# Mixing layer in seven block products per pair of output chunks, with weight sums from DRAM and a fixed queue order into the up-projection

## The chip, the cores and the metric

The kernel runs on one core of a Trainium2 chip. The metric is the device time in microseconds (us) of one execution; lower is better. TensorE (PE) multiplies, VectorE (DVE), ScalarE (ACT) and GpSimd (POOL) do the elementwise work, and the SyncE queue (SP) issues most transfers. Each engine works through its own queue in the order in which the kernel's instructions stand there.

## The reference, cut to what matters

One layer of a hybrid decoder, all in float32, with 1024 tokens, a width of 1024 and a feed-forward width of 2816:

```python
xn = rmsnorm(x, norm_mix_w[l])
proj = xn @ w_in[l]
...
y_da = diff_attention(da_q, da_k, da_v, lam, lam_init, subln_w[l])
y_sw = sliding_window_attention(sw_q, sw_k, sw_v, sinks[l])
merged = jax.nn.sigmoid(g_da) * (y_da @ w_br_da[l]) + jax.nn.sigmoid(g_sw) * (y_sw @ w_br_sw[l])
x = x + merged @ w_mix_out[l]
xn = rmsnorm(x, norm_ffn_w[l])
x = x + conv_ffn(xn, w_up[l], conv_w[l], conv_b[l], w_down[l])
```

The change is about the line `x = x + merged @ w_mix_out[l]`, called mixing here, and about what stands on both sides of it: the merge of the two branches before, the first product of the up-projection (`up`) behind.

## The kernel before

Activations lie transposed: a matrix of 1024 x 1024 is eight chunks of 128 channels x 1024 tokens, and a half is 512 tokens of a chunk. Every float32 operand is split into a high part (a cast by ACT) and a low part (a subtraction by DVE: source less high part); a product of two blocks then takes three matmuls (high x high, high x low, low x high) of 128 x 128 against 128 x 512. In `mm3` these are L215, L216 and L217.

The stages are `project` (L315), `attention` (L544), and in `rest` (L819) the merge, then `mix` (L880), `hidden` with up (L960) and `down` (L1263). A pair of output chunks in project, up and down is already computed by seven block products instead of eight (a Strassen scheme): with the weights' blocks A11, A12, A21, A22 and the activations' blocks B11, B12, B21, B22, the products take sums of weight blocks (S1 to S4) and sums of activation blocks (T1 to T4). In project and up POOL makes the weight sums in SBUF; for down they are made in DRAM by `sums_of` (L82), with copies on SP's queue and accumulating transfers on POOL's.

*Merge.* For each of eight output chunks m, two gates are loaded (gr), multiplied by rstd on POOL (L846) and put through a sigmoid on ACT; PE multiplies the branch weights, DVE multiplies gate and product (L857 and L862), POOL adds the branches (L863, DVE for the last chunk), and the chunk is split (L866, L867) into the operands mh and ml.

*Mixing.* For each output chunk, in the order 0, 4, 1, 5, 2, 6, 3, 7, eight input chunks x two halves x three matmuls = 48 matmuls accumulate in PSUM (sc), DVE adds the result to the residual (L905), ACT stores it (x2d, a transfer issued from ACT's queue, L610), multiplies by the norm's weight (L908) and squares (L917), and POOL adds the squares up (L918, in the tile rstd). After every second chunk `operands` (L924) builds up's operands B11, B21, B22 and T13 from the pair (L943 to L947); T4 and T2 are left as sums in t42 tiles and are split at the start of up. The weights of a chunk are split by ACT (L194) and DVE (L196) ahead of the chunk. A scheduler places most of the instructions; `in_order` makes the instructions of its block keep the written order on the engines that it is given, and is used before from within up's first pair on.

*Start of up.* The column sums of the squares are matmuls against ones (L223); DVE makes the mean (ms, L230), POOL takes the power -0.5 (rs, L232), and PE spreads it over the partitions (L238). The products of up are `product` (L957). The weights of up's first pair are split in `split_pair` (L175).

## Time and profile before

| what | value |
|---|---|
| median of 3 runs (lowest to highest) | 1323.16 us (1323.06 to 1323.33) |
| profiled execution: its time, its span | 1323.83 us, 1322.0 us |
| granted TensorE clock over the span | 0.998 |
| busy PE, DVE, ACT, POOL | 1307.9, 1019.0, 658.0, 476.4 us |
| evictions of mixing (L905), first and last start | 599.5 and 675.7 us |

The page's engine row gives busy time, share of the span and instructions. PEld is the loading of weights, which overlaps the matmuls. In the view of waits a row names an engine and line, what it waited for, and then the total, the count and the longest one in us. In a windows table the engines stand as PE, PEld, DVE, ACT, POOL with their instructions in brackets, then the granted clock, the DMA share and GB/s. In a group of instructions the busy time and the mean in ns follow the bar; in the view of a line or tile it is the least, median and greatest duration in ns.

### The profile page before, as it was taken

The numbers are of one execution on the slowest core, as the hardware profiler recorded it, in microseconds if no ns is written. First come the engines' busy times: TensorE is split into PE (matmuls) and PEld (weight loads), VectorE is DVE, ScalarE is ACT, GpSimd is POOL, SyncE is SP. The second block draws the span as 40 slices with busy tenths as digits, with TensorE's granted clock in tenths as the row PEclk, the third lists the DMA queues.
The fourth block names the chain that finished last, engine by engine and source line by source line (L and its number), as shares of the span: only waits on it lengthen the run. The fifth ranks groups of instructions, "written<-read, shape, count | busy, mean of one in ns | idle before, by whom it ended". The sixth has DMA issues, their size and how long they took to land. (4 is left out here: it accounts for less than half of the span.)

```text
span 1322.0 us, 16947 instructions
## 1 busy us (share of the span) xinstructions
PE 1307.9 (99%) x6210; PEld 1089.6 (82%) x6210; DVE 1019.0 (77%) x1380; ACT 658.0 (50%) x1043; POOL 476.4 (36%) x364
## 2 busy tenths in 40 slices
PE   9999999999999999999999999999999999999997
PEld 7888888888888878888887888888888888888886
DVE  8847775289888976446678988888988898896855
ACT  8532232276667765334445545445454544554543
POOL 0446652000111015661427667656766632000002
PEclk9999999999999999999999999999999999999999
DMA  7344343976544236334433546745554127953534
GB/s 262 116 142 158 148 154 127 259 188 178 153 124 143 85 120 223 144 112 149 137 112 123 184 143 153 201 146 137 197 139 124 62 86 259 330 191 118 160 98 147
DMA packets 71586, 205.95 MB, mean 156 GB/s; under 512 B 8016, under 2 KB 15824, under 8 KB 71376
## 3 DMA queue, kind: packets, MB, share of 16 engines
q1 hardware_dynamic: 57472, 176.03, 40.7%
q0 software_dynamic: 2304, 11.54, 4.9%
q10 hardware_dynamic: 11728, 17.31, 3.6%
q8 instruction: 49, 0.80, 0.2%
q14 instruction: 33, 0.27, 0.1%
HBM read 156.08 MB, written 71.83 MB: 172 GB/s over the span
## 5 line engine op out<-in xcount | busy, mean ns | idle before, releaser
L1243 POOL TENSOR_TENSOR us<-us,rstd 128x1024 f32<-128x1024 f32 x42 | 105.3, 2507 | 145.6 <-DVE us L1168 109.8
L196 DVE TENSOR_TENSOR wl<-raw,wh 128x1024 fp32r<-128x1024 f32 (+2 forms) x85 | 97.5, 1148 | 58.8 <-ACT wh L194 49.2
L194 ACT CAST wh<-raw 128x1024 fp32r<-128x1024 f32 (+2 forms) x85 | 74.2, 874 | 120.2 <-PE y L1313 50.7
L145 DVE TENSOR_TENSOR sl<-sf,sh 128x1024 fp32r<-128x1024 f32 x42 | 105.2, 2506 | 3.4 <-ACT sh L138 3.4
L232 POOL TENSOR_TENSOR rs<-ms,mhalf 128x8 f32<-128x8 f32 (+2 forms) x9 | 14.2, 1576 | 240.3 <-DVE ms L230 234.1
L1180 DVE SCALAR_TENSOR_TENSOR c<-us,vecs,c 128x1024 f32<-128x1024 f32 x76 | 95.6, 1279 | 0.7
L1313 PE MATMUL y<-h,wh 128*128 128x512 f32 (+1 forms) x324 | 95.2, 377 | 0.0
L1313 PE MATMUL d<-h,wh 128*128 128x512 f32 x264 | 81.3, 389 | 0.0
L215 PE MATMUL g<-xh,wh 128*128 128x512 f32 x176 | 71.0, 404 | 1.5 <-ACT g L618 1.5
L217 PE MATMUL g<-xh,wl 128*128 128x512 f32 x176 | 70.3, 399 | 0.0
L216 PE MATMUL g<-xl,wh 128*128 128x512 f32 x176 | 70.3, 399 | 0.0
L1313 PEld LDWEIGHTS y<-h,wh 128*128 128x128 f32 x324 | 59.4, 188 | 11.1
L1313 PE MATMUL y<-h,wl 128*128 128x512 f32 (+1 forms) x162 | 60.9, 376 | 0.0
L693 DVE CUSTOM_DVE_ANT_0 L<-sc,bias 128x128 f32<-128x128 f32 (+7 forms) x64 | 47.7, 751 | 17.1 <-PE sc L689 14.0
L672 POOL MEMSET aT<- 128x128 f32 x32 | 6.2, 206 | 151.9 <-PE t L718 98.1
L694 ACT ACTIVATE L<-L,sm 128x128 f32<-128x128 f32 (+7 forms) x64 | 49.6, 778 | 19.9 <-DVE sm L693 17.3
L1313 PEld LDWEIGHTS d<-h,wh 128*128 128x128 f32 x264 | 49.6, 188 | 10.3
L846 POOL TENSOR_TENSOR gr<-gr,rstd 128x1024 f32<-128x1024 f32 x16 | 40.3, 2523 | 46.3 <-DMA gr<-gd 46.1
L1313 PE MATMUL d<-h,wl 128*128 128x512 f32 x132 | 51.5, 390 | 0.0
L138 ACT CAST sh<-sf 128x1024 fp32r<-128x1024 f32 x42 | 44.3, 1054 | 11.7 <-POOL sf L124 7.6
L216 PE MATMUL sc<-ml,wh 128*128 128x512 f32 x128 | 49.9, 390 | 0.0
L689 PE MATMUL sc<-u,u 128*128 128x512 f32 (+2 forms) x192 | 49.9, 359 | 0.0
(438 smaller groups left out, 4180.4 us busy)
## 6 DMA issues: line engine op xcount, KB each, us to landing
u<-qd SPq DMA_DIRECT2D x72, 256.0 KB, 6.5
raw<-in_w_up SPq DMA_DIRECT2D x23, 512.0 KB, 3.9
raw<-in_w_in SPq DMA_DIRECT2D x22, 512.0 KB, 3.7
hd<-c SPq DMA_DIRECT2D x22, 512.0 KB, 4.0
sdP<-in_w_down POOLq DMA_DIRECT2D x16, 704.0 KB, 8.6
rv<-in_w_up SPq DMA_DIRECT2D x21, 512.0 KB, 3.6
hc<-hd SPq DMA_DIRECT2D x33, 256.0 KB, 5.1
gr<-gd SPq DMA_DIRECT2D x16, 512.0 KB, 3.5
```

The lines of the kernel that those rows point to most:

```text
L145: self.nc.vector.tensor_tensor(lo, src, hi.bitcast(F32), ALU.subtract)
L194: self.hi = nc.scalar.copy(wh, raw)
L196: self.lo = (eng or nc.vector).tensor_tensor(wl, raw, wh.bitcast(F32), ALU.subtract)
L215: nc.tensor.matmul(ps, wh[:, kc + o, :], ah, start=first and n == 0, stop=False)
L216: nc.tensor.matmul(ps, wh[:, kc + o, :], al, start=False, stop=False)
L217: nc.tensor.matmul(ps, wl[:, kc + o, :], ah, start=False, stop=last and n == len(kcs) - 1)
L689: nc.tensor.matmul(sc[:, lo + n0:lo + n1], qs, k[c][part][:, n0:n1], start=part == 0, stop=part == 1)
L693: nc.vector.tensor_tensor_reduce(L[:, :w], sc[:, lo:lo + w], self.bias[:, o:o + w], slope, 3e38, ALU.add, ALU.min, s[:, 0:1])
L694: nc.scalar.activation(L[:, :w], L[:, :w], AF.Exp, bias=s[:, 0:1], scale=-1.0, accum_out=s[:, 1:2] if c else self.s0[:, i:i + 1])
L1180: nc.vector.scalar_tensor_tensor(c, us[:, 2 - n:T + 2 - n], cw[2 - n], c, ALU.mult, ALU.add)
L1243: i = (nc.vector if m % NF == 0 else nc.gpsimd).tensor_tensor(us[:, 2:], us[:, 2:], self.rstd, ALU.mult)
L1313: nc.tensor.matmul(ps, v[:, k - k0, :], x, start=start and k == i == 0, stop=k == HK - 1 and i == 2, skip_group_check=True)
```

## The change

Mixing goes over to seven products as well, for the pairs of output chunks (0, 4) and (1, 5), then (2, 6) and (3, 7). One product is 12 matmuls (four input chunks x three) into one half; there are 28 products, counted here 1 to 28 in the order in which PE takes them, 14 for each round. In a round with chunks a and b, two products share a weight unit: B11 and B21 of a (1, 2), of b (3, 4); T2 and T1 of a (5, 6), of b (7, 8); T3 and B22 of a (9, 10), of b (11, 12); T4 of a and b (13, 14). The second round has 15 to 28. Products of one chain accumulate in one bank of PSUM, and the bank's intermediate states are added to several output blocks.

- `mix_sums` makes the sums of w_mix in DRAM during project: 32 transfers of 256 KB, 16 copies on SP and 16 accumulating ones on POOL, four per pair.
- The merge runs over the chunks 0, 4, 1, 5, 2, 6, 3, 7, its gates lie in other buffers, and behind each second chunk `mix_operands` splits the six operands of the pair. In the last chunk DVE evicts and adds half by half.
- From the last merge chunk's second branch through mixing into up, `in_order` fixes DVE, ACT and POOL in the written order. Weights are prepared by `ahead(1)`, one unit ahead.
- In mixing, DVE adds one product in three to the residual tiles straight from PSUM; of the others ACT copies the bank and POOL adds (`copied`). Squares, stores (now by half chunks), norm weights, and up's operands (`put`, `t13`, `t4`) follow at once. The first pair of up is loaded, summed and split within the second round.
- up's first pair is computed in the fixed order, and `down` takes its buffers for loaded chunks from tiles that mixing left.

The core of the diff:

```diff
+    def mix_sums(self):
+        row = lambda m, r: self.w_mix[m].rearrange("p k c -> p (k c)")[:, r * H2:(r + 1) * H2]
+        copy = lambda n, src: lambda m: nc.sync.dma_start(self.sm[m][:, n], src(m))
+        add = lambda n, o, r: lambda m: nc.gpsimd.dma_start(self.sm[m][:, n], row(m + o, r), accum_op=ALU.add)
+        for step in (copy(1, lambda m: row(m + 4, 0)), copy(2, lambda m: row(m + 4, 0)), add(1, 4, 1), add(2, 0, 0),
+                     copy(0, lambda m: self.sm[m][:, 1]), add(0, 0, 0), copy(3, lambda m: self.sm[m][:, 0]), add(3, 0, 1)):
...
             for j, ms in enumerate(self.pairs):
                 w = self.next_w()
+                for _ in range(4):
+                    with tc.issue_after(self.sync), tc.issue_after(self.sum):
+                        next(sums, None)
...
-                for m in range(KC):
+                for m in self.mix_order:
...
-                    (nc.vector if m == KC - 1 else nc.gpsimd).tensor_tensor(gs[0], gs[0], gs[1], ALU.add)
-                    a = mp.tile([P, T], F32R, name=f"mh{m}")
-                    b = mp.tile([P, T], F32R, name=f"ml{m}")
-                    nc.scalar.copy(a, gs[0])
-                    nc.vector.tensor_tensor(b, gs[0], a.bitcast(F32), ALU.subtract)
+                    nc.gpsimd.tensor_tensor(gs[0], gs[0], gs[1], ALU.add)
+                    res[m] = gs[0]
+                    if m > 3:
+                        self.mix_operands(m - 4, "B11", "B21", "B22", "T13", "N2", "T4", ga=res[m - 4], gb=res[m])
+                self.last = {i.engine: None for i in (self.hi.ins, self.lo.ins, self.pow.ins)}
+                with self.in_order(self.last):
+                    ga, gb = res[3], gs[0]
+                    for hf in range(2):
...
+                        nc.vector.tensor_tensor(g, g, ps, ALU.mult)
+                        nc.vector.tensor_tensor(x, x, g, ALU.add)
...
+    def mix_operands(self, k, *names, ga, gb):
...
+        for name in names:
+            if name == "T13":
+                tt(b11, b11, b12, ALU.subtract)
+                tt(b12, b22, b12, ALU.subtract)
+            elif name == "N2":
+                stt(b22, b22, -1.0, b11, ALU.mult, ALU.subtract)
+            elif name == "T4":
+                stt(b21, b22, -1.0, b21, ALU.mult, ALU.subtract)
+            hi, lo = self.split(*self.M[name, k], {"B11": b11, "B21": b21, "B22": b22, "T13": ga, "N2": b22, "T4": b21}[name])
...
+        def post(m, hf):
+            x = h2(X[m], hf)
+            if hf in begun:
+                sq = self.tl(stp, [P, H2], "s")
+                nc.scalar.activation(sq, x, AF.Square)
+                gt(h2(acc, hf), h2(acc, hf), sq, ALU.add)
...
+            nc.scalar.dma_start(self.x2d[m, :, hf * H2:(hf + 1) * H2], x)
+            if m > 3:
+                norm_w(m, hf)
...
+        with self.in_order(self.last):
+            self.mix_operands(3, "B11", "B21", "B22", "T13", "N2", "T4", ga=ga, gb=gb)
...
+            for a in (0, 2):
...
+                wa = self.wq.pop(0)
+                c1[a] = bank(n1[0])
+                run(c1[a], wa, 0, "B11", True)
+                self.ahead(1)
...
+                run(c2[a], wa, 1, "B21", True)
+                copied(c1[a], a, 0)
+                wb = self.wq.pop(0)
...
+                tt(h2(X[b], 1), h2(X[b], 1), c3[b], ALU.add)
+                post(b, 1)
+                t13(a)
+                if a:
+                    put("B22", b, h2(t42[b], 1))
+                    self.low(pair, "g")
+                    self.sums(pair, "sb")
+                run(c1[b], v, 1, "T4", False)
...
-            with tc.high_priority(400):
-                w0 = self.split_pair(*pair)
+            with self.in_order(self.last):
+                self.whole(pair, "sa")
+                self.ends[0]()
+                self.whole(pair, "sb")
+                self.ends[1]()
+                self.whole(pair, "v")
+            w0 = pair["w"]
...
+                    order = self.in_order(self.last)
+                    order.__enter__()
                     for k in range(4):
                         hi, lo = self.split(*(xc2.tile([P, T], F32R, name=f"T42_{k}{p}") for p in "hl"), self.t42[k])
...
-                            with tc.high_priority(400):
-                                rs = self.rstd_cols(ssq, 8, D)
+                            rs = self.rstd_cols(ssq, 8, D)
+                    order.__exit__(None, None, None)
```

How the change stands on the engines is shown at three places. A name that ends in h or l is a high or low part; wh, wl are the parts of a plain weight, sh, sl those of a weight sum; yr, ga and g with numbers are gate tiles, x the residual tiles, n banks of PSUM. The first place is DVE at the passage from the merge into mixing, before. The two wl are the weights of the last merge chunk and of mixing's first, ml the low halves of merge chunks 6 and 7:

```order
L196 TENSOR_TENSOR wl_5592<-raw_5588,wh_5590 128x1024
L867 TENSOR_TENSOR ml_5585<-gr_5521,mh_5584 128x1024
L857 TENSOR_TENSOR gr_5594<-gr_5594,sc_5602 128x1024
L862 TENSOR_TENSOR gr_5598<-gr_5598,g_5628 128x512
L862 TENSOR_TENSOR gr_5598<-gr_5598,g_5642 128x512
L863 TENSOR_TENSOR gr_5594<-gr_5594,gr_5598 128x1024
L196 TENSOR_TENSOR wl_5718<-raw_5714,wh_5716 128x1024
L867 TENSOR_TENSOR ml_5658<-gr_5594,mh_5657 128x1024
L905 TENSOR_TENSOR x_1010_5712<-x_1010_5712,sc_5720 128x1024
```

And in the change, from the last add of the merge on (t_1045 and sf hold the parts of B11 and B21 there); wl_5850 is the second weight of mixing, which product 3 reads:

```order
L906 TENSOR_TENSOR g_1040_5693<-g_1040_5693,yr_5697 128x512
L914 TENSOR_TENSOR t_1045_5787<-g_1032_5624,t_1045_5787 128x512
L914 TENSOR_TENSOR sf_5788<-g_1040_5693,sf_5788 128x512
L914 TENSOR_TENSOR mB223l<-g_1040_5693,mB223h 128x512
L923 TENSOR_TENSOR g_1032_5624<-g_1032_5624 128x512
L924 TENSOR_TENSOR g_1032_5624<-g_1040_5693,g_1032_5624 128x512
L914 TENSOR_TENSOR mT133l<-g_1032_5624,mT133h 128x1024
L926 SCALAR_TENSOR_TENSOR g_1040_5693<-g_1040_5693,g_1032_5624 128x512
L914 TENSOR_TENSOR mN23l<-g_1040_5693,mN23h 128x512
L928 SCALAR_TENSOR_TENSOR g_1040_5693<-g_1040_5693 128x512
L914 TENSOR_TENSOR mT43l<-g_1040_5693,mT43h 128x512
L208 TENSOR_TENSOR wl_5850<-raw_5622,wh_5848 128x1024
```

Before, one low half of 128x1024 stood behind the weight of mixing's first chunk; now ten steps of the last operand set stand between that add and the low half of mixing's second weight, while the first weight's is ahead of them.

The second place is ACT at the turn from mixing's first round to its second, before (the same kind of stretch, between the weights of chunks 4 and 1):

```order
L194 CAST wh_5856<-raw_5854 128x1024
L908 ACTIVATE xw_5832<-x_1016_5773,vecs 128x1024
L917 ACTIVATE t_5846<-x_1016_5773 128x512
L876 CAST B_0h<-xw_5832 128x512 x2
L876 CAST T_0h<-xw_5770 128x1024
L917 ACTIVATE t_5849<-x_1016_5773 128x512
L610 DMA x2d<-x_1016_5773 128x1024
L194 CAST wh_5923<-raw_5921 128x1024
```

And in the change; x_5832 and x_5828 are residual tiles of chunks 1 and 0, c_6016 a t42 tile, and wh_6130 the weight of products 17 and 18:

```order
L993 ACTIVATE s_6084<-x_5832 128x512
L998 DMA x2d<-x_5832 128x512
L986 ACTIVATE x_5828<-x_5828,vecs 128x512
L913 CAST T_0h<-x_5828 128x1024
L993 ACTIVATE s_6107<-x_5830 128x512
L998 DMA x2d<-x_5830 128x512
L986 ACTIVATE c_6016<-x_5830,vecs 128x512
L206 CAST wh_6130<-raw_6037 128x1024
L913 CAST B_0h<-c_6016 128x512
```

The weight's cast stands behind the squares, the half-chunk stores and the operand's cast of the products before.

The third place is DVE at the start of up, before; wl_6322, sl_6314 and sl_6318 are the last three low halves of up's first pair of weights:

```order
L905 TENSOR_TENSOR x_1068_6221<-x_1068_6221,sc_6223 128x1024
L175 TENSOR_TENSOR wl_6322<-raw_6207,wh_6320 128x512
L175 TENSOR_TENSOR sl_6314<-sf_6209,sh_6312 128x1024
L175 TENSOR_TENSOR sl_6318<-sf_6210,sh_6316 128x1024
L944 TENSOR_TENSOR xw_6203<-xw_6274,xw_6203 128x512
```

And in the change; L1120 is the eviction of product 26, L1128 and L1133 those of 27 and 28, and wl_6399 the low half of up's first weight:

```order
L1120 TENSOR_TENSOR x_6116<-x_6116,n_1119_6281 128x512
L1006 TENSOR_TENSOR x_6112<-x_6112 128x512
L1007 TENSOR_TENSOR x_6112<-t_1124_6330,x_6112 128x512
L914 TENSOR_TENSOR mT130l_5135<-x_6112,mT130h_5134 128x1024
L1013 TENSOR_TENSOR t_1124_6330<-t_1124_6330,x_6112 128x512
L914 TENSOR_TENSOR mN22l_5133<-x_6379,mN22h_5132 128x512
L157 TENSOR_TENSOR wl_6399<-raw_6353,wh_6398 128x1024
L1128 TENSOR_TENSOR x_6114<-x_6114,n_1053_5826 128x512
L914 TENSOR_TENSOR mB220l_5139<-t_1124_6330,mB220h_5138 128x512
L1017 TENSOR_TENSOR t_1124_6330<-t_1124_6330 128x512
L1133 TENSOR_TENSOR x_6238<-x_6238,n_1054_5827 128x512
```

Before, the low halves of up's weights came directly behind the last eviction (and the first of them ahead of it); now that of the first weight stands behind the eviction of product 26 and five steps of operands, and those of the sums behind product 28's.

More of the change, by code (lines that the diff above doesn't have):

```diff
@@ L887, in mix @@
         xc = self.xctx2.enter_context(tc.tile_pool(name="xc", bufs=1, reuse_waits="tile"))
-        self.B = {}
-        xt = {(n, k, p): xc.tile([P, w], F32R, name=f"{n}_{k}{p}") for n, w in (("B11", H2), ("B21", H2), ("T13", T), ("B22", H2)) for k in range(4) for p in "hl"}
+        own = {n: [xc.tile([P, T if n == "T13" else H2], F32R, name=f"{n}_0{p}") for p in "hl"] for n in ("B11", "B21", "B22", "T13")}
         self.sfp = self.xctx2.enter_context(tc.tile_pool(name="sfp", bufs=2, reuse_waits="tile")), "sf"
-        self.t42 = [self.tl(self.cpl, [P, T], "c") for _ in range(2)] + [self.tl(self.sfp[0], [P, T], "t42", bufs=1)]
@@ L963, in hidden @@
             e = ctx.enter_context
-            first = ExitStack()
-            self.psF = first.enter_context(tc.tile_pool(name="psE", bufs=1, space=PSUM, reuse_waits="tile"))
+            first = self.first
             xc2 = e(tc.tile_pool(name="xc2", bufs=1, side="right", reuse_waits="tile"))
```

282 lines of the change are left out of this document (223 added, 59 removed).

## The prediction

> **What bounds the kernel now.** I read the page first, then what PE (TensorE) waits for, then the mixing stage by windows, then the price of each form of instruction there. The page's engine row and its chain:
>
> ```profile
> PE 1307.9 (99%) x6210; PEld 1089.6 (82%) x6210; DVE 1019.0 (77%) x1380; ACT 658.0 (50%) x1043; POOL 476.4 (36%) x364
> ...
> PE 45%; issue 0%; POOLq 0%; POOL 0%; DVE 0%; ACT 0%
> ```
>
> PE is busy 1307.9 of 1322.0 us. So a matmul that goes is worth its whole time, and a wait that comes is paid in full. All waits of PE by the view of waits, mixing and the start of up (L957) among them:
>
> ```profile
> PE g L215 <- ACT g L618: 1.5, 4, 0.5
> ...
> PE d L238 <- POOL rs L232: 1.1, 1, 1.1
> PE d L223 <- ACT c L1301: 0.8, 1, 0.8
> PE n L957 <- ACT wh L138: 0.7, 1, 0.7
> ...
> PE n L957 <- ACT s L1128: 0.2, 1, 0.2
> ```
>
> There is nothing from mixing (L215 to L217 into sc) in it, and 0.9 us at the start of up. The evictions of mixing (L905) give the pace:
>
> ```profile
> L905 DVE TENSOR_TENSOR x<-x,sc x8: 1220/1222/1222, 599.5 to 675.7; 128x1024 f32<-128x1024 f32 x8
> ...
>   PE sc L217: 25.7, 8
> ```
>
> Seven intervals in 76.2 us, 10.89 us each for 48 matmuls: 0.2268 us a matmul (the groups' mean of 389 ns holds the overlap of neighbours). DVE sat idle 25.7 us ahead of these evictions: in this stage everybody waits for PE. The windows of mixing, of the last operands, and of the first pair of up:
>
> ```profile
> 600.00:620.00 20.00, 20.00 (x90) 16.53 (x90) 12.09 (x12) 8.27 (x11) 2.97 (x2) 1.00 0.46 142
> ...
> 676.00:700.00 24.00, 24.00 (x120) 20.23 (x118) 19.82 (x22) 12.49 (x17) 12.10 (x7) 1.00 0.17 64
> 700.00:720.00 20.00, 19.10 (x83) 15.06 (x82) 19.45 (x18) 13.58 (x18) 11.73 (x10) 1.00 0.48 161
> ```
>
> After the stretch and its length stand PE, weight loads, DVE, ACT and POOL, then the granted clock. DVE has 8 us of 20 free in mixing, and next to nothing from 676 on (19.82 of 24, 19.45 of 20). The change puts its new work just ahead of that place.
>
> **The prices.** DVE: a weight's low half (128x1024), a subtraction of two SBUF tiles and a low half (128x512):
>
> ```profile
> L196 DVE TENSOR_TENSOR wl<-raw,wh 128x1024 fp32r<-128x1024 f32 x7 | 8.5, 1218 | 0.0
> ...
> L944 DVE TENSOR_TENSOR xw<-xw,xw 128x512 f32<-128x512 f32 x4 | 2.8, 690 | 0.3
> ...
> L877 DVE TENSOR_TENSOR B_0l<-xw,B_0h 128x512 fp32r<-128x512 f32 x3 | 2.0, 684 | 1.5 <-ACT B_0h L876 1.5
> ```
>
> ACT: a square and a cast of 128x512, a cast of 128x1024; and what a store issued from ACT holds it up (by tile x2d):
>
> ```profile
> L917 ACT ACTIVATE t<-x 128x512 f32<-128x512 f32 x14 | 8.4, 618 | 0.0
> L194 ACT CAST wh<-raw 128x1024 fp32r<-128x1024 f32 x7 | 7.4, 1055 | 33.1 <-PE sc L216 33.1
> ...
> L876 ACT CAST B_0h<-xw 128x512 fp32r<-128x512 f32 x3 | 1.7, 607 | 0.0
> ```
>
> ```profile
> L610 ACTq DMA_DIRECT2D x2d<-x x8: 326/326/327, 600.8 to 680.5; - x8
> ```
>
> POOL: the add to the sum of squares, and the power; then a DVE subtraction that met POOL's adds:
>
> ```profile
> L918 POOL TENSOR_TENSOR rstd<-rstd,t x14: 1290/1660/1838, 613.4 to 682.2; 128x512 f32<-128x512 f32 x14
> ```
>
> ```profile
> L232 POOL TENSOR_TENSOR rs<-ms,mhalf x1: 2566/2566/2566, 691.3 to 691.3; 128x8 f32<-128x8 f32 x1
> ```
>
> ```profile
> L943 DVE TENSOR_TENSOR xw<-xw x4: 693/1666/1667, 604.2 to 669.8; 128x512 f32<-128x512 f32 x4
> ```
>
> And for copies from PSUM on ACT, and for the handover from PE's last matmul to DVE (the mean of squares behind its column sums):
>
> ```profile
> L618 ACT COPY g<-g x22: 567/587/589, 241.6 to 502.2; 128x512 f32<-128x512 f32 x22
> ```
>
> ```profile
>   PE n L223: 0.2, 1
> ```
>
> So I use DVE 0.69 (128x512) and 1.22 (128x1024), ACT 0.61 and 1.05, 0.33 for a store on ACT, 1.3 to 1.66 for POOL's add; and keep for the bounds that a DVE subtraction can take 1.67 beside POOL. The Trainium skill (page "SBUF — State Buffer", section "SBUF: two separate sides") says that a DVE instruction with two SBUF inputs and a GpSimd instruction that reads SBUF lock each other out for the whole instruction. The 693 against 1667 ns agree. By that rule, if six of the dozen such steps on the last two walks below met an add, the sum would be some 6 us higher (0.98 each), an estimate; the walks are made without it.
>
> **Removed.** Mixing had 8 x 48 = 384 matmuls; it now has 28 products of 12 = 336. 48 x 0.2268 = 10.9 us off PE: **-10.9**.
>
> **Project: the weight sums.** 16 copies on SP and 16 accumulating transfers on POOL, in eight steps of four, a step to a pair. The nearest row is the same thing for w_down, beside a window of project:
>
> ```profile
> L87 POOL DMA_DIRECT2D sdP<-in_w_down x16: 809/1069/1150, 785.4 to 995.4; - x16
> ```
>
> ```profile
> 120.00:140.00 20.00, 20.00 (x90) 16.57 (x89) 13.96 (x14) 5.29 (x7) 12.50 (x8) 1.00 0.37 133
> ...
> 560.00:580.00 20.00, 20.00 (x90) 16.55 (x89) 8.22 (x7) 7.97 (x8) 13.89 (x5) 1.00 0.26 94
> ```
>
> Four at 1.07 are 4.3 us in a POOL that has 7.5 us of 20 free, and the DMA share is 0.37. They hide: **0**; if POOL's sums come late for the next pair, up to +2.
>
> **Merge: three of the four operand sets.** Each set is 10 DVE steps (9 x 0.69 + 1.22 = 7.4 us) and 6 casts on ACT (4.1 us), every second chunk, in 21.8 us; the second row above (a stretch of merging) shows DVE 8.22 and ACT 7.97 of 20 busy. There is room: **0**, up to +3 if a gate tile comes free late. No gain, since PE does not wait there now.
>
> **Entry into mixing.** The first place shown with the change: behind the last merge chunk DVE must do the whole operand set of chunk pair 3 before it may split w_mix[1]. PE has the two products of w_mix[0] meanwhile, 24 x 0.2268 = 5.4 us. From the end of the last merge matmul: handover 0.2; seven DVE steps of 0.69 (second half of the eviction and its add, lows of B11, B21, B22, two subtractions) to 5.0; T13 cast 1.05, low 1.22: 7.3; subtraction 0.69, N2 cast 0.61, low 0.69, subtraction 0.69, T4 cast 0.61: 10.6; then ACT casts w_mix[1], 1.05: 11.6, and DVE makes its low half, 1.22: 12.8. Product 3 can have its first two matmuls at 11.6 and the third at 12.8: PE waits 12.8 - 5.4 - 0.5 = **+6.9** (6 if steps are some 10% shorter and overlap better, 8 with two collisions). Before, that weight was split ahead of the last chunk's own split, and nothing waited.
>
> **Body.** Weights are prepared one unit (two products, 5.4 us) ahead, in a fixed queue, so whatever stands ahead of a cast delays it. The worst place is the turn from the first pair of chunks to the second, shown for ACT: after product 12 DVE evicts (0.69), ACT squares, stores, multiplies (0.62 + 0.33 + 0.61), DVE subtracts twice (1.38), ACT casts T13 (1.05), DVE makes its low (1.22), subtracts (0.69) and evicts product 13 (0.69), ACT squares, stores, multiplies (1.56), casts the weight of products 17 and 18 (1.05), DVE makes its low (1.22): 11.1 us. It starts 2.9 us late, since in the steps before DVE waits for ACT's cast of the weight ahead. PE has products 13 to 16 and two matmuls: 48 + 2 at 0.2268, 11.3 us. 14.0 - 11.3 = +2.7. The next casts come late by their spacing on ACT, each span being what ACT waits for DVE plus its own steps. To the weight of product 19: 2.7 (the low half and three DVE steps behind the turn's cast, less one cast) and 3.8 (square, store, multiply, copy, cast of 1.05, cast of B22 ahead): 6.5 us. To those of 21 and 23: 1.9 (low half, eviction) and 5.0 (square, store, copy, multiply, three casts of 0.61, the weight's 1.05): 6.9 us each. PE takes 5.4 a unit, so it waits 1.0, 1.1 and 1.6 us (the first matmuls of a unit need only the high half). 2.7 + 3.7 = **+6.4**. Lower end 0: without the 2.9 us of lateness the first chain just fits. Upper end 10, with three or four collisions of 1 us. To product 25 ACT has 3.5 us: no wait.
>
> **Entry into up.** The second place shown for DVE. After product 26 PE has 28 matmuls (6.35 us) until the low half of up's first weight is needed. DVE evicts product 26 (0.69), ACT squares, stores, multiplies (1.56), DVE subtracts twice (1.38), ACT casts T13 (1.05), DVE: low 1.22, subtraction 0.69, low of B22 of chunk 3 0.69, and only then that weight's low half 1.22: 8.5 us. +2.2. Then B21 of chunk 2 comes behind the eviction of product 27: +0.9. The column sums need the last add of squares, POOL's last in this queue: eviction of product 28 ends 13.5 us after product 26, square 0.62, add 1.3 to 1.66: 15.5, while PE is there after 8.5 + 0.9 + 17 x 0.2268 = 13.2: +2.4 with the handover. The power then stands behind the nine remaining low halves (seven of 1.22, two of 0.69: 9.9), four subtractions (2.8) and a wait for a cast (1.05), 13.7 us, and takes 2.57: ready at about 30.0. PE's other 62 matmuls of the pair and the sums last from 15.7 to 30.4: 0. Sum 5.5; the 0.9 us that PE waits there now go: **+4.6** (2, if half of it is covered; 9.5, if the five DVE steps ahead of the weight collide with POOL's adds).
>
> Down only changes which tiles it loads into, with the same count: 0. **Sum:** -10.9 + 0 + 0 + 6.9 + 6.4 + 4.6 = +7.0 us. The profiled execution took 1323.83 us (span 1322.0) and the median of the runs is 1323.16; the sum is a difference, so I set it on the median: 1330.2 us. The ends together: -10.9 + 6 + 0 + 2 = -2.9, and -10.9 + 8 + 10 + 9.5 + 2 = +18.6.
>
> **Rivals.** About 0.2% (2.6 us) is what a measurement of this kernel can tell from no change.
>
> *The cold clock (slower still).* A long gap may also slow the matmuls behind it. The only gaps of note in this trace are at its start:
>
> ```profile
> 1.46 3.59 PE L368 MATMUL t<-xl 128*128 128x512 f32 x8 [1.46 <-DVE xl L366]
> 6.22 0.50 PE L341 MATMUL t<-xh,wh 128*128 128x512 f32 x1 [1.17 <-ACT wh L376]
> 6.56 0.40 PE L342 MATMUL t<-xl,wh 128*128 128x512 f32 x1
> ```
>
> The first eight matmuls took 3.59 us, 0.449 each instead of 0.227, and after 1.17 us of idle they were soon quick again. The entry into mixing would be the first gap of over 6 us within the run. If it costs the same eight slow matmuls, that is 8 x 0.222 = 1.8 us, twice that if up's entry does it too: 1332.0 to 1333.8. The Trainium skill (page "TensorE: Matmul & The Clock Gate", section "What's actually happening") says that the array's clock halves after an idle window of about 3.4 us and returns after as long a busy one. The start of the trace agrees, no row of it shows a gap inside the run that long. Chance 0.27.
>
> *Faster: the wait at the entry is the only one.* While PE waits 6.9 us there, POOL and SP go on, and ACT and DVE have the room that the first window shows (12.09 and 8.27 of 20), so the later chains could fit. Then -10.9 + 6.9 = -4.0: 1319.2. This needs the waits in the body and at up's entry together to stay under 2.3 us (with up's present 0.9 gone). Against it: the order lets no weight be split more than a unit early, and the chain into up starts from PE's own product 26, so a head start does not help it. Chance 0.13.
>
> *The gain just cancels.* The body's chains fit, the two entries stay: -10.9 + 6.9 + 4.6 = +0.6, 1323.8. For it: each body wait is a small difference of long sums. Chance 0.15.
>
> **The numbers.** My forecast without a cold clock has 0.45, with it 0.27: slower 0.72, same 0.15, faster 0.13. The forecast's own range is 1326 to 1337. The range 1321.0 to 1339.0 takes in the cancelling case, the cold clock and most of the unknown collisions, and leaves the faster case and the far upper end out.
>
> **What would show it.** In the new profile: mixing's matmuls 336; a PE wait of 6 to 8 us on the low half of w_mix[1] (wl L208) at product 3, by far the largest of all; waits of 1 to 3 us on wh or wl at products 17 to 23; waits at up's start on a low half (L157) and of the column sums on POOL (L994). No wait at product 3 above 4 us would break the main step; a sum of the later waits under 2.3 us would make the forecast's sign wrong; slow matmuls of 0.45 us behind the first gap would prove the cold clock.

## The result, and the profile after

The changed kernel takes 1352.88 us (median of 4 runs, 1352.48 to 1353.02) against 1323.24 us for the kernel before beside it (1323.06 to 1323.98). The ratio is 1.0222, 95% interval 1.0205 to 1.0240: 29.6 us slower. Forecast were +7.0 us and a range up to 1339. The sign was right, the size four times too small.

The profiled execution took 1353.02 us (span 1351.2), 29.2 more than that of before. The page's engine row and the row of granted clocks:

```profile
PE 1309.8 (97%) x6162; PEld 1086.0 (80%) x6162; DVE 1041.5 (77%) x1428; ACT 679.4 (50%) x1087; POOL 507.2 (38%) x392
...
PEclk9999999999999999999889999999999999999999
```

PE has the 48 matmuls less (6162 for 6210), and yet is busy 1.9 us longer. Work that shrank and takes longer has run slower: two of the forty slices show a clock of 8 tenths. The waits of PE that were not there before, by the view of waits (us in total, times, the longest):

```profile
PE n L1178 <- ACT wh L206: 8.8, 2, 5.7
PE n L1178 <- DVE wl L157: 5.8, 1, 5.8
PE n L1178 <- DVE wl L208: 5.1, 1, 5.1
PE g L227 <- DVE yr L893: 4.6, 3, 2.1
PE n L1178 <- ACT s L1355: 1.7, 1, 1.7
...
PE n L235 <- POOL rstd L994: 0.9, 1, 0.9
```

Before, this part of the kernel had 0.9 us of waits at two places in up (and PE was busy 50.00 of 50 us in each window from 500 to 700); now it has 28.5, with both of these places still among them. The windows of 50 us lay them out, from the merge (the first two rows) through mixing into up. After the stretch and its length stand PE, weight loads, DVE, ACT, POOL, then the granted clock:

```profile
500.00:550.00 50.00, 47.99 (x211) 38.87 (x210) 30.13 (x28) 22.17 (x25) 33.78 (x14) 1.00 0.51 188
550.00:600.00 50.00, 47.13 (x205) 37.85 (x203) 40.16 (x46) 18.93 (x24) 23.18 (x8) 1.00 0.36 128
600.00:650.00 50.00, 41.50 (x168) 33.34 (x168) 24.05 (x25) 22.56 (x33) 15.97 (x11) 0.93 0.36 116
650.00:700.00 50.00, 39.35 (x148) 30.59 (x148) 34.10 (x33) 24.04 (x38) 24.43 (x18) 0.84 0.42 133
700.00:750.00 50.00, 45.51 (x200) 36.59 (x201) 39.91 (x43) 28.18 (x36) 23.42 (x17) 0.96 0.35 120
```

PE loses 2 to 3 us per window in the merge, and 8.5, 10.7 and 4.5 us in the next three, where the clock also falls. The clock takes about 41.50 x 0.07 + 39.35 x 0.16 + 45.51 x 0.04 = 11 us (the matmuls that follow each other by 0.43 instead of 0.23 us add up to 10.6). By the timeline of PE, the first matmul behind each large gap, with the idle time ahead of it and what ended it:

```profile
605.69 0.79 PE L1178 MATMUL n<-mB110h,wh 128*128 128x512 f32 x1 [5.70 <-ACT wh L206]
...
650.29 0.79 PE L1178 MATMUL n<-mB110h,wh 128*128 128x512 f32 x1 [3.06 <-ACT wh L206]
...
676.36 0.79 PE L1178 MATMUL n<-mT130h,wl 128*128 128x512 f32 x1 [5.05 <-DVE wl L208]
...
700.58 0.80 PE L1178 MATMUL n<-B_0h,wl 128*128 128x512 f32 x1 [5.75 <-DVE wl L157]
```

These are product 3, product 17, product 23 and up's first product. Stage by stage, mixing starts 5.9 us late; it lasts 12.3 us longer (10.9 less work, 13.8 of waits, the rest half clock); up's first pair lasts 9.8 us longer; 1.2 come later. By kind: -10.9 for the matmuls, +5.9 up to the end of the merge (4.9 of it waits), +13.8 of waits in mixing, +7.2 at up's entry (5.75 + 0.91 + another 0.56), +1.5 behind it (1.71 at L1355 and 0.73 at a weight's cast, where there were 0.18 and 0.72 before), +11 of half clock. That makes 28.5; 0.7 us I cannot place.

Windows of 3 us show the half clock itself: PE stands still, then has 7 and 9 matmuls in 3 us where 14 is the rate, then the clock is back:

```profile
597.00:600.00 3.00, 3.00 (x14) 1.00 1.02 418
600.00:603.00 3.00, 0.00 (x0) 1.00 0.26 101
...
606.00:609.00 3.00, 2.96 (x7) 0.50 0.28 90
609.00:612.00 3.00, 3.00 (x9) 0.50 0.70 199
612.00:615.00 3.00, 3.00 (x15) 0.99 0.38 147
```

Why the gap at product 23 is 5.05 us and not 1.6 stands in its timeline:

```profile
666.16 1.67 POOL L994 TENSOR_TENSOR rstd<-rstd,s 128x512 f32<-128x512 f32 x1 [4.30 <-ACT s L993]
...
666.64 1.74 DVE L914 TENSOR_TENSOR mB210l<-x,mB210h 128x512 fp32r<-128x512 f32 x1
...
668.31 1.78 DVE L914 TENSOR_TENSOR mB211l<-x,mB211h 128x512 fp32r<-128x512 f32 x1
...
670.61 4.62 POOL L1041 TENSOR_TENSOR x<-x,s 128x512 f32<-128x512 f32 x3 [1.07 <-ACT s L1040]
...
670.72 1.71 DVE L1160 TENSOR_TENSOR c<-c 128x512 f32<-128x512 f32 x1
...
672.35 1.75 DVE L914 TENSOR_TENSOR mB212l<-x,mB212h 128x512 fp32r<-128x512 f32 x1
...
674.03 2.28 DVE L208 TENSOR_TENSOR wl<-raw,wh 128x1024 fp32r<-128x1024 f32 x1
```

Five DVE steps of this stretch lie beside a POOL addition and take 1.71 to 2.28 us instead of 0.69 and 1.22: some 5 us, on the queue that ends with the low half PE waits for. (The one step between them that starts while POOL is idle, at 670.01, takes 0.68.) The merge has the same with larger tiles, in two stretches of its timeline:

```profile
534.69 2.87 POOL L875 TENSOR_TENSOR yr<-yr,rstd 128x1024 f32<-128x1024 f32 x1 [3.42 <-DMA yr<-gd]
...
535.22 2.89 DVE L926 SCALAR_TENSOR_TENSOR yr<-yr,ga 128x512 f32<-128x512 f32 x1
...
546.41 6.18 POOL L875 TENSOR_TENSOR yr<-yr,rstd 128x1024 f32<-128x1024 f32 x2
...
547.60 2.72 DVE L914 TENSOR_TENSOR mB111l<-ga,mB111h 128x512 fp32r<-128x512 f32 x1
...
550.36 2.78 DVE L923 TENSOR_TENSOR ga<-ga 128x512 f32<-128x512 f32 x1
```

The POOL steps here are not additions but the gates' multiplications by rstd (L875), which the kernel before had too (L846). Three operand steps that I put at 0.69 took 2.72 to 2.89 beside them; the eviction L893 stands behind them, and PE waits for its PSUM bank.

### The profile page after: what moved, and what is told of

Its sections match the earlier page's. It is cut to its first block, busy times and chain, and to the rows that moved or that the text cites. A ratio compares the mean times of both kernels' runs of the same rounds, so it can differ in the third digit from the quotient of the medians.

```text
span 1351.2 us, 17095 instructions
## 1 busy us (share of the span) xinstructions
PE 1309.8 (97%) x6162; PEld 1086.0 (80%) x6162; DVE 1041.5 (77%) x1428; ACT 679.4 (50%) x1087; POOL 507.2 (38%) x392
## 5 line engine op out<-in xcount | busy, mean ns | idle before, releaser
L206 ACT CAST wh<-raw 128x1024 fp32r<-128x1024 f32 (+2 forms) x91 | 80.4, 885 | 87.7 <-PE y L1551 50.7
L157 DVE TENSOR_TENSOR sl<-sf,sh 128x1024 fp32r<-128x1024 f32 x44 | 107.6, 2448 | 5.2 <-ACT sh L150 5.2
L157 DVE TENSOR_TENSOR wl<-raw,wh 128x1024 fp32r<-128x1024 f32 (+1 forms) x23 | 27.6, 1201 | 30.4 <-ACT wh L150 30.4
L139 POOL TENSOR_TENSOR sf<-raw,sf 128x512 f32<-128x512 f32 x22 | 49.0, 2226 | 0.0
```

The costliest lines, as they stand in the source:

```text
L157: self.nc.vector.tensor_tensor(lo, src, hi.bitcast(F32), ALU.subtract)
L206: self.hi = nc.scalar.copy(wh, raw)
```

## The experiments

The theory after this reading has two causes: the written order lets chains of DVE and ACT steps end behind PE, and DVE steps that meet POOL's steps stretch these chains; half clock behind each gap comes on top. The rivals: one cause alone (the order, the collisions, or the clock), or a single late wait that the rest only follows. Each ratio is against the kernel before, run beside it.

**The clock by itself, first try.** Useless matmuls fill the four gaps.

```diff
+                fill(bank(6 if a == 0 else 7), 24 if a == 0 else 13)
...
+                    fill(bank(0), 22)
...
+            fill(bank(0), 25)
```

> The changed kernel with 84 matmuls of no use (19.05 us at 0.2268) put into the four long gaps of PE: 24 ahead of product 3, 13 ahead of 17, 22 ahead of 23, 25 ahead of up's first product. They write an idle PSUM bank that nobody reads, and PE's order in mixing is fixed. Theory 1 (the gaps cost their wait and then about 3 us of half clock each): the granted clock stays at 1.0 and the time falls by 9 to 13 us, to 1340 to 1344, though PE does more. Theory 2 (the matmuls behind a gap are slow because their operands or the engines beside them are): no change, 1352 to 1354. Theory 3 (what PE waits for is itself waiting for PE): the gaps open again behind the added matmuls, 1358 to 1372.

Measured: 1349.17 us, ratio 1.0192 (1.0177 to 1.0208): outside all three expectations. The clock was held at 1.00 up to 700 us, yet the time fell by 3 to 4 us only. Up's first pair then lost part of it:

```profile
700.00:705.00 5.00, 2.39 (x16) 1.92 (x14) 2.69 (x4) 3.69 (x6) 1.27 (x1) 0.93 0.92 283
705.00:710.00 5.00, 5.00 (x16) 4.13 (x16) 3.85 (x5) 2.74 (x4) 0.00 (x0) 0.50 0.08 31
```

PE now comes early, waits 2.6 us at the column sums for POOL's last square, and goes cold there instead. The 11 us of half clock can thus not all be won back by a warm PE: where a late chain sets the time, slow matmuls partly lie in the shadow of that chain.

**The clock by itself, second try.** Three PE gaps put into mixing of the kernel before, where nothing is late.

```diff
+            if i in (2, 4, 6):
+                with tc.high_priority(400):
+                    s = self.tl(self.st, [P, 8], "ms")
+                    self.gap = nc.vector.tensor_scalar(s, ps[:, T - 8:], 1.0, 0.0, ALU.mult, ALU.add).ins
+                    for _ in range({2: 1, 4: 3, 6: 12}[i]):
+                        self.gap = nc.vector.tensor_scalar(s, s, 1.0, 0.0, ALU.mult, ALU.add).ins
...
```

> The kernel before, with three gaps of PE made on purpose in its mixing: the first matmul of the third, fifth and seventh output chunk waits for small DVE steps that read the product before (about 2.9, 4.7 and 9.5 us by the rows of the steps that stand between). The results are unchanged. Theory 1 (a gap costs its length, and a long one some 3 us of half clock more): the granted clock falls to 0.5 behind the second and third gap and stays there for some 6 us, the time is 1323.5 + gaps + about 6. Theory 2 (the slow matmuls of the changed kernel have to do with its own order): matmuls at 0.227 us right behind each gap, 1323.5 + gaps alone.

Measured: 1348.28 us, ratio 1.0187 (1.0172 to 1.0202), +25.0 us. The gaps of 2.69, 5.15 and 10.50 us sum to 18.3, so 6.7 us are left, 2.2 us a gap. Its trace, taken in the fastest of the four runs (1347.43), shows 4.6 us of that as half clock, 1.5 a gap. Each gap has about 3 us of it, the longest no more than the smallest; behind the smallest it begins only some 1.1 us after PE has resumed:

```profile
613.22 0.47 PE L215 MATMUL sc<-mh,wh 128*128 128x512 f32 x1 [2.69 <-DVE ms L910]
613.53 0.39 PE L219 MATMUL sc<-ml,wh 128*128 128x512 f32 x1
...
614.75 0.63 PE L220 MATMUL sc<-mh,wl 128*128 128x512 f32 x1
...
617.64 0.39 PE L215 MATMUL sc<-mh,wh 128*128 128x512 f32 x1
```

A matmul shown with 0.63 comes every 0.43 us, one with 0.39 every 0.23. So the price of such a gap is its length plus some 1.5 to 2 us. How long a gap must be is less sharp than these three suggest; the last section has a gap that went both ways.

**The entry alone.** The weight of products 3 and 4 is split ahead of most of chunk pair 3's operands.

```diff
-            self.mix_operands(3, "B11", "B21", "B22", "T13", "N2", "T4", ga=ga, gb=gb)
+            self.mix_operands(3, "B11", "B21", ga=ga, gb=gb)
+            self.ahead(2)
+            self.mix_operands(3, "B22", "T13", "N2", ga=ga, gb=gb)
...
+                if a == 0:
+                    self.mix_operands(3, "T4", ga=ga, gb=gb)
...
```

> The changed kernel with one part of the order changed: the split of mixing's second weight stands behind the lows of B11 and B21 of chunk pair 3, ahead of its other operands, and T4 of that pair is split later, behind the eviction of product 2. Theory 1 (the entry waits for that one split in the queue, and then for the clock): the 5.7 us gap ahead of product 3 and the 3 us of half clock behind it go, a wait of about 1 us may come at product 5: 1344 to 1346. Rival (the queue of ACT and DVE is full, so what is taken from product 3 is missed at products 5 to 9): 1350 to 1353, with new gaps there.

Measured: 1345.36 us, ratio 1.0162 (1.0145 to 1.0179), as expected. The gap of 5.70 us is gone and with it a cold phase: about 7.5 us. The gaps at products 17 (3.1) and 23 (5.1) and at up (5.7) stay.

**POOL out of the evictions.** The copy from PSUM on ACT and the addition on POOL become one DVE addition straight from PSUM.

```diff
-                    t = self.tl(stp, [P, H2], "s")
-                    nc.scalar.copy(t, bank)
-                    gt(h2(X[m], hf), h2(X[m], hf), t, sign)
+                    tt(h2(X[m], hf), h2(X[m], hf), bank, sign)
```

> The changed kernel with the ten copies on ACT and ten adds on POOL of each round's results replaced by ten DVE adds straight from PSUM (POOL keeps the squares). Theory 1 (in the second round DVE's steps take 1.7 us instead of 0.7 because they meet POOL's adds, and ACT's copies stand ahead of weight casts): the gap ahead of product 23 shrinks from 5.05 us to under 2 and its half clock goes, product 17 stays: 1343 to 1349. Rival (DVE is the bound of mixing, so seven more us of DVE steps make it worse): 1355 to 1362.

Measured: 1345.34 us, ratio 1.0162 (1.0146 to 1.0177), as expected, again 7.5 us. The two large waits of its profile are product 3's and up's; what product 23 had is in the last row:

```profile
PE n L1176 <- ACT wh L206: 8.6, 2, 5.7
PE n L1176 <- DVE wl L157: 6.0, 1, 6.0
...
PE n L1176 <- DVE wl L208: 1.4, 2, 0.8
```

The edit also takes the copies off ACT, so the time alone does not tell the two apart. The trace does: the same five DVE steps ahead of product 23's low half now take 1.74 (still beside an addition of squares), 0.68, 0.69, 0.69 and 1.22 us. DVE got more work (the additions), and these steps got 4.2 us shorter: that is the collision.

**The weight sums alone**, put into the kernel before.

> The kernel before with only the 32 transfers of the weight sums added in project, their results unused. My step for project: 0, so 1323 to 1324. Rival (POOL's descriptor work or the DRAM traffic delays the pairs' own sums and loads): 1325 to 1328.

Measured: 1325.29 us (10 runs), ratio 1.0013 (1.0004 to 1.0023): +1.6 us, 0.5 to 3, the lower end of the rival's range and not my 0. No single wait shows it; about 0.9 of it comes between 583 and 599 us of its trace, behind the stage that has the transfers. The changed kernel's own trace does not show it: its first merge chunk's matmuls start at 501.00 us, those of the kernel before at 501.31.

**One late wait at a time.** Three edits that each mend one place: another PSUM bank for every second eviction of the merge; the low half of up's first weight ahead of the operand steps; the weight of products 17 and 18 ahead of T13 and its eviction.

```diff
-                        ps = self.tl(self.psG, [P, H2], "g")
+                        ps = self.tl(self.psG, [P, H2], "g") if m in self.mix_order[::2] else self.tl(self.psT, [P, H2], "t")
```

> The changed kernel in which the second branch's products of every other merge chunk go to the two PSUM banks that attention left idle, so PE need not wait for DVE's eviction of the chunk before. Theory 1 (merge lost its 5.9 us because DVE's operand steps, some of 2 to 3 us beside POOL's adds, stand ahead of evictions in its queue): PE's three waits on yr (4.6 us) go, mixing starts 4 to 6 us earlier, 1347 to 1349.5. Rival (DVE has too much work there, so the loss shows up at the entry into mixing instead): 1351.5 to 1353.

```diff
                 if a:
                     self.cast(pair, "g")
+                    self.low(pair, "g")
...
```

> The changed kernel in which the low half of up's first weight stands directly behind its cast, ahead of the operands of product 25 and 26's chunks, and the eviction of product 28 stands ahead of the last B21. Theory 1 (the queue order alone makes up's first weight 5.75 us late, and half a clock follows): that gap and the slow matmuls behind it go, 1343.5 to 1347. Rival (the squares, the column sums and the power set the time of the first pair anyway): the wait moves to the column sums and the spread, 1349.5 to 1353.

```diff
-                t13(a)
                 if a:
+                    t13(a)
...
+                    if a == 0:
+                        t13(a)
+                        evict()
```

> The changed kernel in which, at the turn between the two rounds, the weight of products 17 and 18 is split ahead of chunk 0's T13 and of the eviction of product 13. Theory 1 (order alone): the 3.06 us gap ahead of product 17 and its half clock go, 1346 to 1350. Rival (ACT's and DVE's work of the second round is the bound, so what is put off comes back at products 19 to 23): 1351 to 1356.

Measured, in this order: 1351.61 us, ratio 1.0203 (1.0188 to 1.0218); 1352.62 us, 1.0211 (1.0196 to 1.0226); 1351.81 us, 1.0205 (1.0189 to 1.0220). Each time lies in the rival's range, and none is clear of the change's 1.0222 by its interval: the wait goes where the edit is and comes back at the next place. In the merge the waits on yr fall from 4.6 to 1.2 us, but a weight's cast and low half now cost 1.5 and 0.7, some 3 us of half clock follow these two, and mixing begins at 594.28 us (594.26 in the change). At the turn product 17's gap goes and product 19 waits 3.29. Up's is plainest; 5.8 us at the low half (L157) are gone, and in their place stand

```profile
PE n L235 <- POOL rstd L994: 7.9, 1, 7.9
```

So none of these three is the bottleneck that the others only follow.

**All five edits together**, and a second try with other places for them:

> All five edits of order and banks together: entry, sums straight from PSUM, merge banks, up's first weight, the turn. Theory 1 (the seven-product mixing is sound, its loss is waits and the clock behind them): the gains add up, no gap over 1.5 us in mixing, clock 1.0 throughout, 1317 to 1325, that is level with the kernel before or up to 0.5% faster. Rival (the elementwise work is the bound of the stage): not under 1330.

> The kernel with all five edits (e8_all), with the two places mended that still showed long waits: in up's entry the evictions of products 27 and 28 and their squares stand ahead of chunk 2's T13, which follows the first weight sum; at the turn T4 and the eviction of product 14 wait until the weight of products 19 and 20 is split; and B11 of chunks 2 and 3 is split later, where DVE is idle. Theory 1: the 8.1 us gap at up's column sums and the 2.6 us ahead of product 19 go, with the half clock behind them: 1318 to 1325. Rival (the elementwise work of the second round, DVE busy 2.00 of 2 us there, is the bound): the waits come back at products 21 to 28, 1329 to 1336.

Measured: 1335.98 us, ratio 1.0090 (1.0073 to 1.0107), and 1337.47 us, 1.0106 (1.0091 to 1.0121). Both are 15 to 17 us faster than the change. The first is 11 short of its expectation, with a wait of 8.1 us at the column sums; the second lies above both of its ranges, with 2.9 us there and others of up to 2.5 us elsewhere. The entry and the evictions from PSUM alone won 7.5 us each, so my other reorderings added next to nothing: each step that I drew ahead made another late.

**No written order.** Nothing but the fixed queue order of mixing is taken out; the scheduler places the same instructions.

```diff
-        with self.in_order(self.last):
+        with nullcontext():
```

> The changed kernel without the fixed order in mixing: from the last operand set to the end of mixing the scheduler places ACT's, DVE's and POOL's instructions; nothing else is changed. It puts mixing's second weight five steps into the last operand set instead of behind its ten, and the low half of up's first weight right behind the eviction of product 26. Theory 1 (the written order makes the gaps at the two entries): the first falls from 5.7 to 1 to 3 us, the second goes, products 17 and 23 stay: 1340 to 1347. Rival (the seven products simply bring more elementwise work than these engines can place): 1350 to 1356.

Measured: 1333.57 us, ratio 1.0075 (1.0058 to 1.0092): 19.3 us faster than the change, better than expected. So the written order is the largest part of the loss that one edit removes; no other single edit won more than 7.5 us. How much of the 19.3 is order alone stays open, since another order also changes which DVE steps meet POOL's. What is left is 4.6 us in the merge, 4.3 on low halves in mixing and 2.0 us at B22 of chunk 2, with the clock at 0.83 in 650 to 700.

**Both causes together.** The last edit with the evictions straight from PSUM, the second bank in the merge, and the merge's addition (L894) on DVE; then also without the fixed order in up's first weight sums.

> The changed kernel without the fixed order in mixing (as e12_free), and without POOL's part in the stage: sums straight from PSUM by DVE (as e3_psum), the merge's adds on DVE, and the second pair of PSUM banks in the merge (as e5_merge). POOL keeps the gates and the squares. Theory 1 (order and the collisions of DVE with POOL are two separate causes): the gains add up, merge waits under 1.5 us in all, no wait over 2 us in mixing, clock 1.0 in mixing: 1319 to 1326. Rival (with DVE given 20 us more work, DVE becomes the bound): not under 1330.

> As e13_free_psum, with the fixed order taken from up's first weight sums too (they are split where the scheduler puts them). If up's entry still waits in e13 for the order of those splits: 1 to 4 us faster than e13. If it waits for the squares, the column sums and the power: the same within 1 us.

Measured: 1323.28 us (11 runs), ratio 0.9988 (0.9979 to 0.9997); then 1322.11 us (11 runs), 0.9983 (0.9974 to 0.9992), too close to tell apart. The first is in its time range, and the merge's waits came down to 0.5 us, but a wait of 3.0 us stayed in mixing and the clock was 0.86 in 650 to 700, which the expectation had ruled out. The loss is gone, but 9 of the 10.9 us are still missing. The second one's trace has two waits left at the same operand, and the reason ahead of them:

```profile
662.71 0.69 DVE L1126 TENSOR_TENSOR x<-x,n 128x512 f32<-128x512 f32 x1 [0.64 <-PE n L1176]
663.19 6.38 POOL L994 TENSOR_TENSOR rstd<-rstd,s 128x512 f32<-128x512 f32 x4
...
663.32 1.72 DVE L1006 TENSOR_TENSOR x<-x 128x512 f32<-128x512 f32 x1
...
664.96 1.77 DVE L914 TENSOR_TENSOR mN22l<-x,mN22h 128x512 fp32r<-128x512 f32 x1
...
666.65 1.78 DVE L1007 TENSOR_TENSOR x<-t,x 128x512 f32<-128x512 f32 x1
...
668.46 1.66 DVE L1013 TENSOR_TENSOR t<-t,x 128x512 f32<-128x512 f32 x1
```

POOL adds four squares in a row (6.38 us); four DVE steps beside them take 1.66 to 1.78 us, and PE waits 1.28 and 3.00 us for B22 of chunk 2. Behind that the clock is 0.50 to 0.58 for about 10 us.

**The last collision.** The additions of squares also go to DVE; and as a control, both moves (merge additions and squares on DVE) in the kernel before.

```diff
-                gt(h2(acc, hf), h2(acc, hf), sq, ALU.add)
+                tt(h2(acc, hf), h2(acc, hf), sq, ALU.add)
```

> e14_freeh with the adds of the squares on DVE instead of POOL. Theory (collisions): a DVE step that met such an add took about 1.0 us longer, the add itself costs DVE 0.69, so the four steps ahead of B22 of chunk 2 shrink by some 4 us and that operand is ready about 3 to 4 us earlier; the two waits of 1.3 and 3.0 us fall to under 1 us in all, the clock stays up behind them (it lost about half of 10 us), and the time falls by 6 to 10 us, to 1312-1316 us. Rival (DVE is full there, so its own adds cost what the collisions did): the waits stay within 1 us of what they are, 1320-1323 us.

> The kernel before with the same two moves, the adds of the gates in merge and of the squares on DVE instead of POOL, nothing else. Theory: PE waits for neither of them there (its waits are 0.9 us at the start of up), so 1322.5-1324.5 us, no change. Rival (the moves are a gain in themselves): under 1321 us, and then part of the gain of the freely placed version belongs to them and not to the seven products.

Measured: 1317.38 us (1314.78 to 1319.76, 5 runs), ratio 0.9946 (0.9933 to 0.9960); the control 1323.94 us (11 runs), ratio 0.9998 (0.9989 to 1.0007). The same places in the faster one's timeline, waits and windows:

```profile
667.74 0.68 DVE L1006 TENSOR_TENSOR x<-x 128x512 f32<-128x512 f32 x1
...
668.95 0.68 DVE L1007 TENSOR_TENSOR x<-t,x 128x512 f32<-128x512 f32 x1
669.55 0.68 DVE L994 TENSOR_TENSOR rstd<-rstd,s 128x512 f32<-128x512 f32 x1
```

```profile
PE sc L229 <- DVE wl L208: 2.3, 1, 2.3
...
PE n L1176 <- DVE mB220l L914: 1.2, 1, 1.2
```

```profile
650.00:700.00 50.00, 47.87 (x221) 38.93 (x220) 43.64 (x54) 27.46 (x37) 21.10 (x14) 1.00 0.35 116
```

An addition that DVE does itself costs it 0.68; met on POOL it cost 1.0 more per step. The waits on B22 fell from 4.3 to 1.2 us, the clock stays at 1.00, and the seven products are worth 7.1 us of their 10.9 (5.3 to 8.9 by the interval, 6.6 by the medians). The control shows that the moves alone are worth nothing in the kernel before, so the gain is not theirs. The first expectation was 1312 to 1316; 1.4 us of it did not come. The 2.3 us of wait at a weight in the merge are one more collision: that low half took 3.39 us instead of 1.22, beside a gate multiplication (L875), which stayed on POOL.

## Why the prediction was right or wrong

- **Removed, -10.9: as forecast** in the count of instructions (6162); the last experiment gets 7.1 us of it.
- **Weight sums, 0 to +2: within its bounds.** The 0 of the sum was +1.6 (0.5 to 3.0) by itself.
- **Merge, 0 to +3: wrong, +5.9.** The step that failed is "There is room", read from busy time over a window (8.22 and 7.97 of 20). Room on average says nothing about a queue: the new operand steps stand ahead of the eviction in DVE's queue, beside POOL's 128x1024 steps, and took up to 2.89 us each. A second PSUM bank alone did not bring mixing forward, so the bank is only where the wait shows; with the merge's additions on DVE as well, 0.5 us of waits were left there.
- **Entry into mixing, +6.9: right in its chain.** From mixing's first matmul the cast ended after 11.4 us (forecast 11.6) and the low half after 12.6 (12.8). PE waited 5.70 us for the cast (wh L206) and, after two matmuls at half clock, some 0.25 for the low half. Two of the signs named for it missed: the large wait is on the cast and not on the low half, a little under 6, and it is not the largest by far, for up's is 5.75. That it is one of two causes and not the only one (the faster rival) is shown by the other gaps.
- **Body, +6.4: the kind of wait right, a price wrong.** Product 17 came at 3.06 (forecast +2.7). Products 19 and 21 (+1.0 and +1.1; the walk's own spacings less 5.4 would give 1.1 and 1.5) did not wait: the casts came 5.9 and 6.6 us apart (forecast 6.5 and 6.9), and PE itself was some 2.8 us slower at half clock behind product 17. Product 23 waited 5.05 (+1.6), and not for the cast on ACT that the walk followed, which had ended at 670.04, but for the low half on DVE, 674.03 to 676.31. The mis-sized term is the price of a DVE step: 0.69 in the walks, 1.7 beside POOL. I had the row (693 and 1666 ns) and kept it for the upper end only. The Trainium skill's rule of the lock (page "SBUF — State Buffer", section "SBUF: two separate sides") says it outright: a DVE instruction with two SBUF inputs and a GpSimd instruction that reads SBUF block each other for a whole instruction. The trace agrees: the merge's evictions (L893), with one input from PSUM, kept 0.67 to 0.69 in all 14 cases, the one at 541.73 wholly beside a POOL multiplication (541.59 to 544.07). POOL's new additions (L1041) are part of the change, so collisions were its likeliest case, not a bound.
- **Up's entry, +4.6: right place, too small.** 5.75 at the low half (forecast +2.2). Two subtractions took 1.70 and 1.65, and ahead of them DVE stood idle 2.80 for ACT, which had another chunk's multiplication and the cast of that weight (0.71 and 1.03) to do before this chunk's square and multiplication; the walk had left both out. B21 did not wait (+0.9); 0.91 at the column sums (+2.4), 0.56 at the spread (0). The 0.9 us taken off was a misreading: those two waits stood 27 and 39 us after up's first product, behind its first pair, and the change left them there, 1.71 and 0.73 now. So +8.7 in all.
- **Sum: the cold clock was a rival and should have been a term.** It gave 1.8 us for each of two gaps. Four gaps made PE cold, and cost about 11 us of half clock, 6 us long behind products 3 and 17; by itself a gap cost 1.5 to 2.2 us. How much of the 11 could be won back stays open: 3 to 4 us came back when the clock was held up to the column sums, and PE then went cold there. The Trainium skill (page "TensorE: Matmul & The Clock Gate", section "What's actually happening") gives an idle window of about 3.4 us. The runs differ: 2.69 us were enough here, and even 2.04 us in some runs (below). Apart from this, the upper end of the range left out the merge's own +3.

From the forecast's +7.0 to the 29.2 of the profiled run, then: the merge +5.9, the entry -1.2, the body +1.7, up +4.1, the clock +11; 0.7 is not placed.

## What to carry to other kernels

Walk a chain with the price that its steps have in the company they will have: where the change puts work on POOL, take the colliding price (here 1.7 us for 0.69) for every DVE step with two SBUF inputs beside it, and ask whether DVE doing the addition itself isn't cheaper. When PE has no slack, every wait of 3 us or more cost its length plus 1.5 to 3 us of half clock here, and one of 2 us may. And read room from the queue, in its order, not from the busy share of a window; where many short chains meet, mending one late wait only shows the next.

## What the runs showed of the hardware

- Where the clock falls is not a matter of the gap's length alone. The merge's wait of 2.04 to 2.06 us for yr is the same in seven traces, whose kernels differ only behind it. In three (the change, the first try with the clock, no written order) the clock stays at 1.00 behind it; in four (the entry alone, POOL out of the evictions, up's first weight, the turn) some 3 us of half clock follow. First the change, then the entry alone:

```profile
554.92 0.50 PE L227 MATMUL g<-yh,wh 128*128 128x512 f32 x1 [2.05 <-DVE yr L893]
555.25 0.39 PE L228 MATMUL g<-yl,wh 128*128 128x512 f32 x1
```

```profile
554.79 0.57 PE L227 MATMUL g<-yh,wh 128*128 128x512 f32 x1 [2.04 <-DVE yr L893]
555.16 0.63 PE L228 MATMUL g<-yl,wh 128*128 128x512 f32 x1
```

- In the traces of this case, from the merge to up's second pair, half clock followed every gap of 2.55 us or more. A gap of 2.32 us in the last kernel's merge had none. Short gaps had it where more idle time or the column sums lay beside them: 1.49 and 0.66 us, 1.4 us apart (the second bank in the merge), and 1.28 us ahead of the column sums (POOL out of the evictions).
- The eleven runs of the second freely placed version fall in two groups by the granted clock over the span: 0.992 or 0.993 in seven (1322.10 to 1322.92 us), 0.994 to 0.997 in four (1318.19 to 1320.46). One and the same kernel can thus lose more or less to half clock. At which place is not shown, since only one run, of the first group, has a trace.
- Half clock lasted 3 to 10 us, the longest where more waits or the column sums follow the gap. Behind gaps of 2.0 to 3.1 us it often began only about 1 us or more after PE had resumed.
- A POOL step also grows when it meets DVE: four additions of squares took 6.38 us, 1.6 each, for 1.27 at best.
